# Down projection in seven block products: weight sums kept in eight tiles of their own, rings of six operand pairs

## The chip, the core and the metric

The kernel runs on one core of a Trainium2 chip. Its time is in device microseconds (us), the median over runs of the whole program; "profiled execution" means the one execution whose trace is quoted. The engines are PE (TensorE, matmul; PEld is its weight load), DVE (VectorE), ACT (ScalarE), POOL (GpSimd) and SP (SyncE, which here only issues DMAs). Each engine takes its instructions in the order in which they stand in its own queue.

## What is computed

One layer of a decoder for 2048 tokens of width 1024. Three mixers (dilated attention, a convolution module, a gated linear recurrence) share one input projection and one output projection, and a squared-ReLU MLP follows:

```python
mix = jnp.concatenate([y_attn, y_conv, y_lru], axis=-1)
x = x + jnp.einsum("bsc,cd->bsd", mix, w_out)
h2 = rmsnorm(x, norm2_g)
ff = jnp.square(jax.nn.relu(jnp.einsum("bsd,df->bsf", h2, w_up)))
return x + jnp.einsum("bsf,fd->bsd", ff, w_down)
```

A final RMSNorm ends it. All inputs are float32, and the change is in the last product, `ff @ w_down`, 4096 by 1024.

## The kernel before

**Precision.** Each float32 operand is split into a rounded high part and the remainder (`halves`: a cast on ACT, line 891, then a subtraction on DVE, line 892), and each product is made of three matmuls, high by high, high by low, low by high (lines 1427 to 1429 in the down stage).

**Halves of the tokens.** The tokens are worked in two halves `h` of 1024. Each half goes through the output projection (`outproj`), the up projection (`up`) and the down projection (`down`). The mixers of the second half run beside these stages of the first half: `tick` takes a piece of them after each batch of matmuls. In the profile the down stage of the first half lies at 964 to about 1300 us, that of the second half at 1718 to 2033 us.

**Seven products.** The down projection is cut into two-by-two blocks and done with seven block products instead of eight (`PRODUCTS`, in the order 1, 2, 7, 6, 4, 5, 3). The moving operand of a product is a sum of blocks of `ff`, which `up` has written to memory (`fscr`). The stationary operand is a block of `w_down` or a sum of blocks, which is made on DVE during the stage. Each product has eight steps, so the stage has 56 steps `g`; a step has 24 matmuls, on four PSUM banks.

**What a step needs.** For each step there is a pair S (high and low half of the moving operand, 128 by 1024 each) and a pair T (the same of the weights). They lie in 24 places `X(0)` to `X(23)`:

- S has a ring of three pairs (`S_AT`). `s_load(g + 2)` is issued in step g, so it waits until step g - 1 has freed the pair. `s_split(g + 1)` follows in the same step.
- T has a ring of nine pairs (`T_AT`). `ahead(g)` lets the splits run up to eight steps ahead of the matmuls, the sums one further and the loads three.
- Raw blocks of `w_down` come into a ring of seven tiles (`block0` to `block6`), taken in turn.
- `t_sum` makes the weights. Products 7 and 5 subtract one raw block from another (line 1292). Products 6 and 4 add or subtract the two rounded parts of the previous product's weights, two DVE operations each (line 1297).

```python
elif i in (6, 4):
    x = raws[t][0]
    op = nc.vector.tensor_add if i == 6 else nc.vector.tensor_sub
    for y in t_tiles(t - 8)[::-1]:
        op(x, x, f32(y))
```

**What sets the order.** The program text gives a first order and priorities; a scheduler then places each instruction in its engine's queue as early as its own reckoning allows. `with first()` gives the copies out of the PSUM banks (`evac`) priority. They stand at the end of each product: a bank has to be read before the next product writes it. Products 1 and 7 are copied by ACT (lines 1433, 1435), the others are added by DVE (lines 1437, 1440). A queue is not reordered at run time, so a copy waits for whatever stands ahead of it.

**The seam.** During the last product of the first half, `hooks` loads the mixers' results for the next output projection (`act_load`, into places 8 to 15) and splits them (`act_split`).

Of the kernel before, what the change touches and what calls it, by code (L numbers as in the profile page):

```python
# [38 lines left out]
T_AT = ((2, 3), (6, 7), (8, 9), (10, 11), (12, 13), (14, 15), (18, 19), (20, 21), (22, 23))  # L39
S_AT = ((0, 1), (4, 5), (16, 17))  # L40
# [37 lines left out]
def body(tc, xt, w_in, w_v, w_out, w_up, w_down, vecs, lru_wa, lru_wx, consts, out):  # L78
# [1173 lines left out]
    def down_steps(h):  # L1252
        raws, w = {}, {}

        def t_tiles(t):
            return [X(i) for i in T_AT[t % 9]]

        def s_tiles(g):
            return [X(i) for i in S_AT[g % 3]]

        def s_load(g):
            n, kp = divmod(g, 8)
            sh, sl = s_tiles(g)
            nc.sync.dma_start(f32(sl).rearrange("p (k n) -> p k n", k=2),
                              fscr[h, MOVING[PRODUCTS[n]], 2 * kp:2 * kp + 2].rearrange("k p n -> p k n"))
# [5 lines left out]
        def t_load(t, raw=None):  # L1271
# [3 lines left out]
            def block(a, b):  # L1275
                dst = raw()
                src = w_down[16 * a + 2 * kp:16 * a + 2 * kp + 2, :, b * NB:(b + 1) * NB]
                nc.sync.dma_start(dst.rearrange("p (k n) -> p k n", k=2), src.rearrange("k p n -> p k n"))
                return dst

            if i == 1:
                nc.sync.dma_start(f32(t_tiles(t)[1]).rearrange("p (k n) -> p k n", k=2),
                                  down_w[2 * kp:2 * kp + 2].rearrange("k p n -> p k n"))
            else:
                raws[t] = [block(*x) for x in {2: ((1, 0),), 7: ((1, 1), (0, 1)), 6: ((0, 0),), 4: ((1, 0),),
                                               5: ((0, 1), (0, 0)), 3: ((1, 1),)}[i]]

        def t_sum(t):
            i = PRODUCTS[t // 8]
            if i in (7, 5):  # L1290
                x, y = raws[t]
                nc.vector.tensor_sub(x, x, y)
            elif i in (6, 4):
                x = raws[t][0]
                op = nc.vector.tensor_add if i == 6 else nc.vector.tensor_sub
                for y in t_tiles(t - 8)[::-1]:
                    op(x, x, f32(y))

        def t_split(t):
            th, tl = t_tiles(t)  # L1300
            halves(raws.pop(t)[0] if t >= 8 else f32(tl), th, tl)

        return s_tiles, t_tiles, s_load, s_split, t_load, t_sum, t_split
# [335 lines left out]
```

## Time and profile before

| what | value |
|---|---|
| median of 3 runs | 2057.28 us (2055.09 to 2058.45) |
| the profiled execution, its own time | 2052.25 us |
| its span, first to last instruction | 2050.4 us |
| mean granted TensorE clock | 0.993 of full |
| DMA traffic | 416.32 MB, 203 GB/s mean |

The span is the time from the first instruction to the last; 1.85 us of the execution's own time lie around it. A row of a view gives an engine, the source line, the operation with its tiles (written before read), the count, and times. "Idle before" is the time in which the engine had nothing running, with what ended it. PE's matmuls overlap one another, so an idle time of PE is a little less than what was lost there.

### The profile page before, as it was taken

What the parts mean: (1) busy time and instruction counts of PE and PEld (TensorE: products, weight loads), DVE (VectorE), ACT (ScalarE), POOL (GpSimd) and SP (SyncE); (2) the same over time, 40 slices, a digit from 0 to 9 for tenths busy, and PEclk for the clock granted to TensorE, in tenths of its full rate; (3) what the DMA queues carried; (4) which work ended last, traced back from release to release, by engine and by line L of the source; (5) the groups of instructions that cost most, each with busy time, mean ns of one, the idle gap of its engine ahead of it and who ended that gap; (6) DMA issues with size and microseconds to landing.
All of it is one profiled execution on the core that took longest, in us unless ns stands there. A gap on an engine that the chain in (4) does not pass through costs nothing.

```text
span 2050.4 us, 25667 instructions
## 1 busy us (share of the span) xinstructions
PE 1974.6 (96%) x8876; PEld 1588.8 (77%) x8876; DVE 1501.0 (73%) x2009; ACT 1054.1 (51%) x1623; POOL 167.9 (8%) x296
## 2 busy tenths in 40 slices
PE   8999999999999999999998999989999999999997
PEld 6877777887777777887877778767888887887785
DVE  7899865577687667888898997677555555798755
ACT  6144875323667754566665554355545545444331
POOL 0113100000123322000000000100000000000000
PEclk9999999999999999999999999999999999999998
DMA  5555584833786547446995684785444448976734
GB/s 165 175 151 159 175 298 148 276 114 118 240 277 190 185 152 250 152 164 212 338 323 199 203 284 148 239 271 172 151 148 150 152 141 279 328 275 220 251 103 144
DMA packets 208750, 416.32 MB, mean 203 GB/s; under 512 B 26118, under 2 KB 34550, under 8 KB 208556
## 3 DMA queue, kind: packets, MB, share of 16 engines
q1 hardware_dynamic: 189204, 358.27, 52.2%
q0 software_dynamic: 16208, 45.91, 7.5%
q10 hardware_dynamic: 3208, 10.49, 1.5%
q8 instruction: 70, 1.15, 0.2%
q14 instruction: 60, 0.49, 0.1%
HBM read 299.79 MB, written 123.19 MB: 206 GB/s over the span
## 4 chain that ended last, share of the span: by engine, by line
PE 58%; issue 15%; DMA 13%; DVE 9%; ACT 4%; SPq 1%; POOL 1%; DVEq 0%; ACTq 0%; POOLq 0%
PE bank L1113 9%; PE bank L1114 9%; PE bank L1115 9%; PE bank L1428 4%; PE bank L1429 4%; PE bank L1427 4%; DMA rounded<-fscr 4%; PE mm L255 4%; PE mm L261 4%; PE mm L258 4%; DMA pair<-out_w 2%; DVE rounded L892 2%; DVE wide L462 1%; DMA m<-oscr 1%; DMA wraw<-in_w_up 1%
## 5 line engine op out<-in xcount | busy, mean ns | idle before, releaser
L1113 PE MATMUL bank<-rounded,pair 128*128 128x512 f32 x896 | 354.4, 396 | 1.8 <-ACT low L1193 1.7
L1114 PE MATMUL bank<-rounded,pair 128*128 128x512 f32 x896 | 352.9, 394 | 0.0
L1115 PE MATMUL bank<-rounded,pair 128*128 128x512 f32 x896 | 351.0, 392 | 0.0
L891 ACT CAST rounded<-rounded 128x1024 fp32r<-128x1024 f32 (+1 forms) x168 | 160.4, 967 | 316.9 <-DMA rounded<-fscr 256.3
L892 DVE TENSOR_TENSOR rounded<-rounded 128x1024 fp32r<-128x1024 f32 (+1 forms) x168 | 186.3, 1118 | 127.1 <-ACT rounded L891 126.7
L1427 PE MATMUL bank<-rounded,rounded 128*128 128x512 f32 x672 | 264.8, 395 | 10.7 <-ACT v L1435 5.5
L1428 PE MATMUL bank<-rounded,rounded 128*128 128x512 f32 x672 | 264.2, 393 | 5.3 <-DVE rounded L892 5.3
L1429 PE MATMUL bank<-rounded,rounded 128*128 128x512 f32 x672 | 263.3, 392 | 0.0
L1113 PEld LDWEIGHTS bank<-rounded,pair 128*128 128x128 f32 x896 | 168.2, 188 | 42.2 <-issue 2.6
L1115 PEld LDWEIGHTS bank<-rounded,pair 128*128 128x128 f32 x896 | 168.4, 188 | 37.4 <-issue 0.6
L1114 PEld LDWEIGHTS bank<-rounded,pair 128*128 128x128 f32 x896 | 168.4, 188 | 35.9 <-issue 0.7
L255 PE MATMUL mm<-rounded,rounded 128*128 128x512 f32 x496 | 160.8, 400 | 9.5 <-ACT rounded L235 7.5
L261 PE MATMUL mm<-rounded,rounded 128*128 128x512 f32 x496 | 159.7, 397 | 0.0
L1427 PEld LDWEIGHTS bank<-rounded,rounded 128*128 128x128 f32 x672 | 127.0, 189 | 41.3 <-ACT v L1435 6.9
L258 PE MATMUL mm<-rounded,rounded 128*128 128x512 f32 x496 | 158.6, 397 | 0.0
L1428 PEld LDWEIGHTS bank<-rounded,rounded 128*128 128x128 f32 x672 | 127.2, 189 | 34.6 <-DVE rounded L892 8.0
L1429 PEld LDWEIGHTS bank<-rounded,rounded 128*128 128x128 f32 x672 | 127.2, 189 | 26.6
L235 ACT CAST rounded<-raw 128x512 fp32r<-128x512 f32 (+1 forms) x96 | 55.9, 584 | 154.9 <-PE mm L258 110.8
L891 ACT CAST pair<-wraw 128x1024 fp32r<-128x1024 f32 x64 | 67.2, 1050 | 115.0 <-PE bank L1114 112.9
L892 DVE TENSOR_TENSOR rounded<-block,rounded 128x1024 fp32r<-128x1024 f32 x96 | 116.8, 1218 | 12.9 <-ACT rounded L891 12.0
L892 DVE TENSOR_TENSOR pair<-wraw,pair 128x1024 fp32r<-128x1024 f32 x64 | 78.2, 1222 | 62.9 <-ACT pair L891 61.7
L255 PEld LDWEIGHTS mm<-rounded,rounded 128*128 128x128 f32 x496 | 93.8, 190 | 32.0 <-ACT rounded L235 7.9
(320 smaller groups left out, 3773.0 us busy)
## 6 DMA issues: line engine op xcount, KB each, us to landing
block<-in_w_down SPq DMA_DIRECT2D x128, 512.0 KB, 5.7
fscr<-low SPq DMA_DIRECT2D x224, 256.0 KB, 2.2
rounded<-fscr SPq DMA_DIRECT2D x112, 512.0 KB, 4.9
raw<-in_w_in SPq DMA_DIRECT2D x64, 256.0 KB, 3.8
wraw<-in_w_up SPq DMA_DIRECT2D x64, 256.0 KB, 3.0
low<-in_w_up SPq DMA_DIRECT2D x64, 256.0 KB, 3.3
pair<-out_w SPq DMA_DIRECT2D x24, 512.0 KB, 5.9
raw<-in_xt SPq DMA_DIRECT2D x32, 256.0 KB, 3.6
```

The source lines that it names most:

```text
L235: nc.scalar.copy(h, raw)
L255: nc.tensor.matmul(bank, wh[:, sl], ah[:, cols], start=first_, stop=False)
L258: nc.tensor.matmul(bank, wh[:, sl], al[:, cols], start=False, stop=False)
L261: nc.tensor.matmul(bank, wl[:, sl], ah[:, cols], start=False, stop=last_)
L891: nc.scalar.copy(h, raw)
L892: nc.vector.tensor_sub(l, raw, f32(h))
L1113: nc.tensor.matmul(bank, wh[:, sl], hi(x), start=fresh and k == 0, stop=False, **kw)
L1114: nc.tensor.matmul(bank, wh[:, sl], lo(x), start=False, stop=False, **kw)
L1115: nc.tensor.matmul(bank, wl[:, sl], hi(x), start=False, stop=k == KH - 1, **kw)
L1427: nc.tensor.matmul(banks[j], th[:, c], sh[:, x], start=fresh and k0, stop=False, **kw)
L1428: nc.tensor.matmul(banks[j], th[:, c], sl[:, x], start=False, stop=False, **kw)
L1429: nc.tensor.matmul(banks[j], tl[:, c], sh[:, x], start=False, stop=k1, **kw)
```

## The change

S and T each get a ring of six pairs (`S_AT` with six entries, `T_AT` with six). The weight sums get eight tiles of their own, `kept0` to `kept7`, one for each step of a product, and each product's sum is made from the sum of the product before and one raw block: W7 = W(1,1) - W(0,1), W6 = W7 + W(0,0), W4 = W(1,0) - W6. Raw blocks that are only operands of a sum, or that are used as they are in product 3, come into three tiles `second0` to `second2`. In step g the program text asks for: S loads up to step g + 5, S splits up to g + 2, sums up to g + 3, T splits up to g + 2, block loads up to g + 5. The prologue in `up` loads a fourth S pair in place of a seventh T pair.

In the last product of the first half the loads of the mixers' results come later, since places 8 to 15 are now used until step 53, and their splits go in twos. The scratch space for software-made DMA descriptors goes from its default to 4096 bytes, which makes room for the additional tiles.

```diff
-T_AT = ((2, 3), (6, 7), (8, 9), (10, 11), (12, 13), (14, 15), (18, 19), (20, 21), (22, 23))
-S_AT = ((0, 1), (4, 5), (16, 17))
+T_AT = ((2, 3), (6, 7), (8, 9), (10, 11), (12, 13), (14, 15))
+S_AT = ((0, 1), (4, 5), (16, 17), (18, 19), (20, 21), (22, 23))
...
-                raws[t] = [block(*x) for x in {2: ((1, 0),), 7: ((1, 1), (0, 1)), 6: ((0, 0),), 4: ((1, 0),),
-                                               5: ((0, 1), (0, 0)), 3: ((1, 1),)}[i]]
+            if i in (2, 7, 5):
+                block(kept[kp], *{2: (1, 0), 7: (1, 1), 5: (0, 1)}[i])
+            if i in (7, 6, 4, 5, 3):
+                block(second[t % 3], *{7: (0, 1), 6: (0, 0), 4: (1, 0), 5: (0, 0), 3: (1, 1)}[i])
...
             if i in (7, 5):
-                x, y = raws[t]
-                nc.vector.tensor_sub(x, x, y)
-            elif i in (6, 4):
-                x = raws[t][0]
-                op = nc.vector.tensor_add if i == 6 else nc.vector.tensor_sub
-                for y in t_tiles(t - 8)[::-1]:
-                    op(x, x, f32(y))
+                nc.vector.tensor_sub(kept[kp], kept[kp], second[t % 3])
+            elif i == 6:
+                nc.vector.tensor_add(kept[kp], kept[kp], second[t % 3])
+            elif i == 4:
+                nc.vector.tensor_sub(kept[kp], second[t % 3], kept[kp])
...
         def ahead(g):
-            split = min(g + 8, 4 + 3 * (g + 1) // 2, 56)
...
+            for name, to, do in (("s load", 6, s_load), ("s split", 3, s_split), ("sum", 4, t_sum), ("split", 3, t_split), ("load", 6, t_load)):
+                while upto[name] < min(g + to, 56):
+                    do(upto[name])
+                    upto[name] += 1
...
-            if g + 2 < 56 and g:
-                s_load(g + 2)
-            if g + 1 < 56 and g:
-                s_split(g + 1)
             ahead(g)
...
-                act_load(1, 1, 0, 2)
             elif h == 0 and kp == 2:
-                act_load(1, 1, 2, 4)
-                act_load(1, 1, 4, 5)
                 out_load(0, state_["pairs"])
...
-    nc = bacc.Bacc("TRN2", target_bir_lowering=False, num_devices=1)
+    nc = bacc.Bacc("TRN2", target_bir_lowering=False, num_devices=1, dynamic_dma_scratch_size=4096)
```

**Where the queues change.** Three places, all in the first half. In the names, `rounded0`, `1`, `4` and `5` hold the S pairs that matter here, `rounded2` and `3` T pairs.

ACT, at the end of product 7 (step 23), where it copies the four banks into `v`. Before:

```order
L891 CAST rounded4_77<-rounded4_77 128x1024
L891 CAST rounded2_75<-block1_7673 128x1024
L891 CAST rounded2_75<-block2_7674 128x1024
L891 CAST rounded0_73<-rounded0_73 128x1024
L1435 COPY v_7690<-bank0_4017 128x512
L891 CAST rounded3_76<-block3_7675 128x1024
L1435 COPY v_7690<-bank1_4018 128x512
L891 CAST rounded1_74<-rounded1_74 128x1024
L1435 COPY v_7690<-bank2_4019 128x512
L1435 COPY v_7690<-bank3_4020 128x512
```

And with the change:

```order
L891 CAST rounded4_77<-rounded4_77 128x1024
L891 CAST rounded2_75<-kept3_7675 128x1024
L891 CAST rounded4_77<-rounded4_77 128x1024
L235 CAST mr_8634<-m_8560 128x512
L891 CAST rounded3_76<-kept4_7676 128x1024
L1431 COPY v_7691<-bank0_4017 128x512
L1431 COPY v_7691<-bank1_4018 128x512
L891 CAST rounded5_78<-rounded5_78 128x1024
L1431 COPY v_7691<-bank2_4019 128x512
L891 CAST rounded3_76<-kept5_7677 128x1024
L1431 COPY v_7691<-bank3_4020 128x512
```

Before, the S casts of steps 24 and 25 stand ahead of the first and the third copy. Now the S casts of steps 26 and 27 stand ahead of the first and that of step 28 ahead of the third: the casts have moved forward in the queue by as many steps as the ring grew.

SP, at the same place. The S loads in the first list are those of steps 23, 24 and 25 (`rounded4`, `rounded0`, `rounded1`); in the second list those of steps 25 (`rounded1`), 26 and 27 (`rounded4`) and 28 (`rounded5`). `block` and `second` are raw weights. Before:

```order
L1264 DMA rounded4_77<-fscr_117 128x2x512
L1278 DMA block0_7672<-in_w_down 128x2x512
L1264 DMA rounded0_73<-fscr_117 128x2x512
L1278 DMA block1_7673<-in_w_down 128x2x512
L1264 DMA rounded1_74<-fscr_117 128x2x512
```

And with the change:

```order
L1266 DMA rounded1_74<-fscr_117 128x2x512
L1279 DMA second1_7696<-in_w_down 128x2x512
L1279 DMA second2_7697<-in_w_down 128x2x512
L1279 DMA second0_7695<-in_w_down 128x2x512
L1279 DMA second1_7696<-in_w_down 128x2x512
L1266 DMA rounded4_77<-fscr_117 128x2x512 x2
L1266 DMA rounded5_78<-fscr_117 128x2x512
```

One block load stood ahead of each S load; now four, those of steps 28 to 31, stand ahead of three S loads in a row. The last of the three is the one whose cast stands between the copies.

DVE, at the end of product 2 (step 15), where it adds the banks into `z0`. Before:

```order
L1297 TENSOR_TENSOR block3_7675<-block3_7675,rounded5_78 128x1024
L1297 TENSOR_TENSOR block4_7676<-block4_7676,rounded5_78 128x1024
L1297 TENSOR_TENSOR block5_7677<-block5_7677,rounded0_73 128x1024
L557 TENSOR_TENSOR m_8135<-m_8135,m_8205 128x512
L1297 TENSOR_TENSOR block4_7676<-block4_7676,rounded5_78 128x1024
L1440 TENSOR_TENSOR z0_7683<-z0_7683,bank0_4017 128x512
```

And with the change:

```order
L892 TENSOR_TENSOR rounded1_74<-kept3_7675,rounded1_74 128x1024
L1294 TENSOR_TENSOR kept0_7672<-kept0_7672,second0_7695 128x1024
L1294 TENSOR_TENSOR kept1_7673<-kept1_7673,second1_7696 128x1024
L1294 TENSOR_TENSOR kept2_7674<-kept2_7674,second2_7697 128x1024
L557 TENSOR_TENSOR m_8123<-m_8123,m_8192 128x512
L1294 TENSOR_TENSOR kept3_7675<-kept3_7675,second0_7695 128x1024
L1436 TENSOR_TENSOR z0_7684<-z0_7684,bank0_4017 128x512
```

The sums for product 6, eight steps or more ahead of their use, still stand ahead of the first addition of `z0`. They are now one operation each, and each needs a raw block from the ring of three.

## Rows read from the trace of the kernel before

**Rows 1.** The page's busy times of the engines, of the whole span.

```profile
PE 1974.6 (96%) x8876; PEld 1588.8 (77%) x8876; DVE 1501.0 (73%) x2009; ACT 1054.1 (51%) x1623; POOL 167.9 (8%) x296
```

**Rows 2.** Stretches: busy time (instructions) by engine, granted clock, DMA share, GB/s.

```profile
core 0: us, PE busy (x) PEld busy (x) DVE busy (x) ACT busy (x) POOL busy (x), PEclk, DMA share, GB/s
1008.00:1052.00 44.00, 41.81 (x182) 33.73 (x181) 39.10 (x38) 27.07 (x32) 2.14 (x4) 1.00 0.98 348
1104.30:1114.20 9.90, 6.26 (x27) 4.62 (x25) 7.03 (x8) 1.73 (x4) 0.87 (x2) 0.98 0.93 304
1807.00:1851.00 44.00, 44.00 (x196) 36.28 (x195) 41.57 (x40) 18.00 (x21) 0.00 (x0) 1.00 0.70 246
```

**Rows 3.** PE's waits, whole span: for whom, us in total, times, longest.

```profile
PE bank L1428 <- DVE rounded L892: 7.5, 8, 1.4
...
PE bank L1427 <- ACT v L1435: 5.5, 2, 5.2
...
PE bank L1427 <- DVE z L1440: 2.4, 2, 1.9
PE bank L1427 <- DVE u L1437: 2.0, 2, 1.1
PE cb L552 <- ACT mr L235: 1.7, 2, 1.1
...
PE bank L1429 <- DVE rounded L892: 1.5, 2, 1.0
...
PE bank L1427 <- ACT rounded L891: 0.8, 1, 0.8
...
PE bank L1427 <- ACT u L1433: 0.8, 1, 0.8
```

**Rows 4.** Timeline of PE, the start of the second half's down stage.

```profile
1716.31 0.40 PE L1114 MATMUL bank<-rounded,pair 128*128 128x512 f32 x1
1716.54 0.40 PE L1115 MATMUL bank<-rounded,pair 128*128 128x512 f32 x1
1717.76 0.50 PE L1427 MATMUL bank<-rounded 128*128 128x512 f32 x1 [0.82 <-ACT rounded L891]
1718.10 0.40 PE L1428 MATMUL bank<-rounded 128*128 128x512 f32 x1
```

**Rows 5.** Two stretches of the down stages at the lower granted clock.

```profile
1113.89:1120.72 6.83, 4.95 (x12) 3.90 (x13) 5.46 (x6) 4.53 (x6) 0.00 (x0) 0.50 0.29 108
1943.33:1946.75 3.42, 3.42 (x9) 2.64 (x9) 2.70 (x4) 2.90 (x4) 0.00 (x0) 0.50 0.84 293
```

**Rows 6.** Timeline of ACT around the end of product 7, first half.

```profile
1108.28 0.57 ACT L1435 COPY v<-bank 128x512 f32<-128x512 f32 x1
1114.18 1.04 ACT L891 CAST rounded<-rounded 128x1024 fp32r<-128x1024 f32 x1 [5.33 <-DMA rounded<-fscr]
1115.13 1.06 ACT L1435 COPY v<-bank 128x512 f32<-128x512 f32 x2
```

**Rows 7.** Timelines of SP and of POOL just before.

```profile
1103.90 0.37 SPq L1278 DMA_DIRECT2D block<-in_w_down  x1
1104.36 0.46 SPq L1264 DMA_DIRECT2D rounded<-fscr  x1
...
1103.57 0.54 POOL L559 DMA_DIRECT2D m<-gscr  x1
1104.10 0.54 POOL L530 DMA_DIRECT2D m<-lscr  x1
1104.63 0.54 POOL L531 DMA_DIRECT2D mr<-gates_w  x1
```

**Rows 8.** DMA issues: count, KB each, median us to landing.

```profile
block<-in_w_down SPq DMA_DIRECT2D x128, 512.0 KB, 5.7
rounded<-fscr SPq DMA_DIRECT2D x112, 512.0 KB, 4.9
rounded<-mscr SPq DMA_DIRECT2D x8, 512.0 KB, 5.2
```

**Rows 9.** Groups of instructions, 1720 to 2050.4 us: busy, mean ns, idle before.

```profile
L1297 DVE TENSOR_TENSOR block<-block,rounded 128x1024 f32<-128x1024 f32 x32 | 38.1, 1215 | 1.2 <-DMA block<-in_w_down 1.1
```

**Rows 10.** POOL's largest group, whole span, and its DMA's time to landing.

```profile
L591 POOL DMA_DIRECT2D m<-zscr x48 | 28.9, 606 | 397.8 <-PE cb L709 195.9 <-DMA zscr<-z 79.4 <-PE mb L733 41.6
m<-zscr POOLq DMA_DIRECT2D x48, 128.0 KB, 4.0
```

More of the change, by code (lines that the diff above doesn't have):

```diff
@@ L1252, in down_steps, with two @@
     def down_steps(h):
-        raws, w = {}, {}
+        kept, second = [], []
         def t_tiles(t):
-            return [X(i) for i in T_AT[t % 9]]
+            return [X(i) for i in T_AT[t % 6]]
         def s_tiles(g):
-            return [X(i) for i in S_AT[g % 3]]
+            return [X(i) for i in S_AT[g % 6]]
+        def two(a):
+            return a.rearrange("p (k n) -> p k n", k=2)
         def s_load(g):
             n, kp = divmod(g, 8)
-            sh, sl = s_tiles(g)
-            nc.sync.dma_start(f32(sl).rearrange("p (k n) -> p k n", k=2),
+            nc.sync.dma_start(two(f32(s_tiles(g)[1])),
                               fscr[h, MOVING[PRODUCTS[n]], 2 * kp:2 * kp + 2].rearrange("k p n -> p k n"))
@@ L1299, in t_split @@
         def t_split(t):
+            n, kp = divmod(t, 8)
             th, tl = t_tiles(t)
-            halves(raws.pop(t)[0] if t >= 8 else f32(tl), th, tl)
-        return s_tiles, t_tiles, s_load, s_split, t_load, t_sum, t_split
+            halves(f32(tl) if n == 0 else second[t % 3] if PRODUCTS[n] == 3 else kept[kp], th, tl)
+        return s_load, s_split, s_tiles, t_load, t_sum, t_split, t_tiles, kept, second
     def down_prologue(steps):
-        s_tiles, t_tiles, s_load, s_split, t_load, t_sum, t_split = steps
+        s_load, s_split, s_tiles, t_load, t_sum, t_split = steps[:6]
@@ L1334, in down @@
     def down(h, steps, banks, hooks):
-        s_tiles, t_tiles, s_load, s_split, t_load, t_sum, t_split = steps
+        s_load, s_split, s_tiles, t_load, t_sum, t_split, t_tiles, kept, second = steps
         lp = pool(f"early{h}", 1, reuse_waits="tile")
-        raw = ring([lp.tile([P, HS], F32, name=f"block{i}") for i in range(7)])
+        kept.extend(lp.tile([P, HS], F32, name=f"kept{i}") for i in range(8))
         u = lp.tile([P, 4 * NB], F32, name="u")
@@ L1344, in down @@
         vv = rp.tile([P, 4 * NB], F32, name="v")
+        sp = pool(f"second{h}", 1, side="right", reuse_waits="tile")
+        second.extend(sp.tile([P, HS], F32, name=f"second{i}") for i in range(3))
         def part(t, j):
@@ L1562, in hooks @@
                 state_["pairs"] = left_pairs(1)
-                act_load(1, 1, 0, 2)
             elif h == 0 and kp == 2:
-                act_load(1, 1, 2, 4)
-                act_load(1, 1, 4, 5)
                 out_load(0, state_["pairs"])
-            elif h == 0 and kp == 3:
-                act_load(1, 1, 5, 8)
-                out_load(1, state_["pairs"])
-                act_split(1, 0)
             elif h == 0:
-                for n in range(2 * kp - 7, min(2 * kp - 5, 8)):
-                    act_split(1, n)
+                for n0, n1 in ((), ((0, 2),), ((2, 4),), ((4, 5), (5, 6)), ((6, 8),))[kp - 2] if kp < 7 else ():
+                    act_load(1, 1, n0, n1)
+                if kp == 3:
+                    out_load(1, state_["pairs"])
+                else:
+                    act_split(1, 2 * kp - 8)
+                    act_split(1, 2 * kp - 7)
                 if kp == 5:
@@ L1578, in body @@
         tail = down(h, steps, banks, hooks)
+        close(f"second{h}")
         if h:
```

30 lines of the change are left out of this document (9 added, 21 removed).

## The prediction

> **What bounds the kernel now.** I read the page's busy times first, then the busy times by stretch, then PE's waits, then the timelines at the longest wait. The kernel is bound by PE: it is busy 96% of the span [rows 1], and in an undisturbed stretch of the second half's down stage it is busy for all of 44.00 us [rows 2]. The change takes no matmul away. So it can only win back time in which PE stood still, and the question is how much of that belongs to the down stages.
>
> PE's waits of the down stages are those of lines 1427 to 1429 [rows 3]: 7.5 + 5.5 + 2.4 + 2.0 + 1.5 + 0.8 + 0.8 = 20.5 us in 18 waits. The waits of line 1429 (1.5 in two) and the one on an ACT cast (0.8) lie at the starts of the two stages, where the first operands come in; the change leaves these alone. That leaves 18.2 us in 15 waits, of two kinds:
> - **Split waits**, line 1428 on DVE's `rounded`: 7.5 us in 8. The low half of S comes too late for its step.
> - **Copy waits**, line 1427 on `v`, `z` and `u`: 5.5 + 2.4 + 2.0 + 0.8 = 10.7 us in 7. A bank of the finished product has not been read when the next product wants to write it.
>
> A wait costs more than its idle time, because matmuls overlap. Matmuls normally start 0.23 us apart [rows 4]. At a wait of 0.82 the starts are 1.22 apart, which is 0.99 lost, and the next interval is 0.34, another 0.11: 1.10 lost for 0.82, so 0.28 more per wait. And there are two stretches at the lower clock level of 1.2 GHz (granted 0.50) [rows 5]. The first begins inside the longest copy wait, so PE had stood still before it; in it matmuls run for 4.95 us, of which half, 2.5, is lost. The second loses half of 3.42, 1.7. I put both, 4.2, to the copy waits; only the first is shown to belong there.
>
> Split waits: 7.5 + 8 x 0.28 = **9.7**. Copy waits: 10.7 + 7 x 0.28 + 4.2 = **16.9**. Together 26.6 us, 1.3% of the span, can be won.
>
> **How the longest wait comes about.** At the end of product 7, ACT has copied the second bank at 1108.28, then stands 5.33 us for a DMA, casts that S tile at 1114.18 and copies the last two banks at 1115.13, while PE waits 5.2 us for them [rows 3, 6]. The cast is that of step 25, and stands ahead of the copies in ACT's queue, as the order shows. Its load was issued at 1104.36, behind a block load at 1103.90, so it took 9.8 us to land, against a median of 4.9 [rows 7, 8]. Just then POOL issued three loads for the mixers [rows 7], and the DMA engines were busy for 0.93 of 1104.30 to 1114.20 [rows 2]. So this wait is a late landing of an S load, handed on by the order of ACT's queue.
>
> **The change, part by part.**
>
> *S ring of six, splits two steps ahead.* An S load is issued when the matmuls of six steps before are done, instead of three. A step is 24 x 0.23 = 5.5 us, so each operand has 16.5 us more. Even the longest landing, 9.8, is inside that. The split waits go: **-9.7**. Bounds: nothing, if the casts now wait elsewhere for just as long; 9.7. I take all of it, since 16.5 is far over the longest row.
>
> *Copies.* Here the ring does less than it seems. The order shows that the casts moved forward in ACT's queue by the same three steps: ahead of the third copy of product 7 there stood the cast of step 25, whose pair step 22 frees, and now there stands that of step 28, whose pair step 22 frees too. So the S load that the copy waits for starts no earlier than before. What is there for it: from the end of step 22, one step (5.5) and two banks of the next one (12 x 0.23 = 2.8) pass before PE wants the third bank; a cast of 1.04 and a copy of 0.57 [rows 6] come off, which leaves 6.6 us for the landing. The median lands in 4.9 [rows 8], and 9.8 does not fit. Before, one block load stood ahead of each S load on SP, and at the costly place one was issued 0.46 us ahead of it [rows 7], itself waiting for a raw tile. Now the four ahead of it need sums that DVE's queue has some ten steps earlier, so they should be gone when the pair comes free. DVE also has 16 fewer sums in each half, 16 x 1.215 = 19.4 us [rows 9]; they lie beside PE's work and count for nothing themselves, but the copies by DVE (4.4 us of the waits) stand behind less. Bounds: nothing goes (the gate is the same), or all 16.9 goes. I take two thirds, **-11.3**, because the slack is nearer to the common landing than to the rare one.
>
> *Loads.* As many blocks and S tiles as before. In 1008 to 1052 the DMA share was 0.98 [rows 2]; the old text asked there for one and a half T pairs a step, the new one asks for one. I cost this at nothing.
>
> *Raw blocks in three tiles.* A block load now waits for the sum of three steps before. At the end of product 2 four sums for product 6 stand in DVE's queue ahead of the first addition into `z0`, and each needs its raw block. If the last one comes late, PE waits there. The nearest rows are the waits for `z` and `u`, up to 1.9 and 1.1 [rows 3]; before, the same sums took two operations each, so part of the wait is old. I take **+0.9**, bounds 0 and 3 (one raw landing of 5.7 [rows 8] less half a step).
>
> *The seam.* The mixers' loads of the next output projection now wait for steps 50 to 53. They land in 5.2 [rows 8], the splits follow before step 55 ends (two steps, 11 us, less 5.2, a cast of 1.04 [rows 6] and a subtraction, which I take as long as a sum of the same shape, 1.215 [rows 9]): 3.5 us to spare. Cost 0; the bound is one whole landing with both, 7.5.
>
> *PE's queue and POOL's queue* keep their order. The mixers' waits (1.7 in two [rows 3], 2.3 with the extra) may go or stay: 0.
>
> **Sum:** -9.7 - 11.3 + 0.9 = -20.1. The profiled execution took 2052.25 of its own time, with a span of 2050.4, and would take 2032.2. It lies 5.0 under the median of the runs; against the median I forecast 2057.3 - 20.1 = **2037** us.
>
> **Rivals.**
> - *The copies stay as they are.* The gate is the same and the casts stand ahead of the copies, so the copy waits keep their place and price; only the split waits go. 2057.3 - 9.7 = 2047.6. For it: the order. Against it: the slack of 6.6 over the median landing.
> - *Slower: S loads held on SP.* Four block loads stand ahead of three S loads. If the third raw tile comes free late (DVE is busy 39.10 of 44 us in the first half [rows 2]), SP stands, the S loads behind it start late, and bank copies stall at the price of the longest wait, 5.2 + 0.28 + 2.5 = 8.0 each. The old copy waits would stay too. There are 12 product ends with a successor; the point from which it is slower is 9.7 / 8.0, so two of them: -9.7 + 16.0 = +6.3, 2063.6. Against it: at every place that I followed in the order, the sum that frees the tile stands well ahead.
> - *The copies stay and the seam is late.* With the 7.5 at the seam in full: 2047.6 + 7.5 = 2055.1, no change. For it: the first half ends with DVE and ACT on the last operands. Against it: the 3.5 us to spare.
> - *The smaller descriptor ring holds POOL.* POOL issues a DMA in 0.606 us and it lands 4.0 later [rows 10], so some seven are under way at a time. If the ring were too small for that and each had to land first, each would cost 3.4 more; 296 instructions of POOL [rows 1] make 1006 us, and if a tenth of it reaches PE, +100, 2157. The share is a guess; POOL is idle 92% of the time [rows 1]. The Trainium skill, "DMA: Bandwidth & Descriptors", section "SWDGE vs HWDGE vs iDMA", says that the descriptors of DMAs issued from GpSimd are written by software into rings kept in reserved SBUF, and "SBUF — State Buffer", section "SBUF size: 192, 224, or 256?", gives that reserve as 16 KiB per partition; the change leaves 4096 bytes. Neither says what happens when it fills, and no run so far shows a smaller one.
>
> **Numbers.** My forecast 0.58; copies stay 0.22; S loads held 0.09; no change by the seam 0.08; descriptor ring 0.03. The first two are faster: 0.80. No change, within 0.2% or 4.1 us, which is about what a measurement of this kernel can tell: 0.08. Slower: 0.12. The range: its low end is all 26.6 and the mixers' 2.3 gone, 2028; its high end is the split waits alone less the 3 of a late raw block, 2057.3 - 6.7 = 2050. That leaves out the last three cases, 0.20. My own case alone gives 2028 to 2044 (a third of the copy waits gone and 0.9 lost: 9.7 + 5.6 - 0.9 = 14.4, so 2043).
>
> **What would show it.** Right: no waits of line 1428 on DVE inside the stages; copy waits of 6 us or less with their surplus, in fewer than seven; no half-clock stretch at the end of product 7; at most one new wait for `z` at the end of product 2. The same copy waits with the S cast ahead of them mean the first rival. SP's block loads late, with S loads issued right behind them, mean the second. A wait on `rounded` at the second half's `outproj` means the seam. POOL's DMAs 4 us apart mean the ring. I am wrong altogether if the gain comes from other stages, or if the time moves by over 4 us with PE's waits of lines 1427 to 1429 unchanged.

## The result and the profile after

| | kernel before | the change |
|---|---|---|
| median, five runs each on one chip | 2055.09 us (2054.51 to 2058.45) | 2044.68 us (2037.72 to 2047.68) |
| ratio of the times | | 0.9938, 95% interval 0.9914 to 0.9961 |
| once more, 16 and 7 runs | 2052.68 us | 2039.52 us, ratio 0.9935 (0.991 to 0.996) |
| the profiled execution, its own time | 2052.25 us | 2037.72 us (second profile 2039.24) |
| first half's down stage, first to last matmul start | 339.34 us | 330.48 (332.01) |
| second half's down stage | 315.13 us | 306.20 (306.20) |

The ratio makes 0.0062 x 2055.09 = 12.7 us, with 8.0 and 17.7 at the ends of its interval. The two down stages together are 17.8 us shorter in the profile (654.47 to 636.68). The profiled execution, the fastest of the five, is 14.5 shorter than that of the kernel before. Most of the difference between 17.8 and 14.5 lies ahead of the first half's down stage, which begins 3.1 us later (967.80 instead of 964.67); there the program text differs only in the prologue in `up`. In the 14 profiles of this study that start lies anywhere from 963.0 to 972.1, so whole runs vary by several us before the down stages begin. The stage lengths are the finer measure, and they are used below beside the medians.

The page's busy times answer to [rows 1]:

```profile
PE 1966.7 (97%) x8876; PEld 1587.4 (78%) x8876; DVE 1466.1 (72%) x1977; ACT 1053.8 (52%) x1623; POOL 168.4 (8%) x296
```

The same number of matmuls. DVE has 32 instructions less and 34.9 us less, 1.1 us each. The busy times by stretch, where the first and third stretch answer to [rows 2], the second is the place of the longest wait now, and the last is the half-clock stretch behind it, as in [rows 5]:

```profile
core 0: us, PE busy (x) PEld busy (x) DVE busy (x) ACT busy (x) POOL busy (x), PEclk, DMA share, GB/s
1008.00:1052.00 44.00, 42.74 (x189) 34.98 (x188) 33.30 (x34) 24.58 (x29) 2.14 (x4) 1.00 0.99 355
1140.00:1162.00 22.00, 16.54 (x72) 13.33 (x71) 16.33 (x16) 7.99 (x10) 1.62 (x4) 0.98 0.89 293
1807.00:1851.00 44.00, 44.00 (x195) 36.41 (x194) 36.20 (x30) 19.12 (x21) 0.00 (x0) 1.00 0.80 283
1161.14:1164.56 3.42, 3.24 (x8) 2.57 (x9) 1.92 (x4) 3.16 (x5) 0.00 (x0) 0.50 0.85 305
```

The DMA engines are as full in 1008 to 1052 as before (0.99, before 0.98), and DVE has 33.30 instead of 39.10 there. PE's waits in the down stages answer to [rows 3]; lines 1427 to 1429 are now 1423 to 1425:

```profile
PE bank L1423 <- DVE u L1433: 5.5, 1, 5.5
...
PE bank L1423 <- DVE z L1436: 1.6, 2, 1.3
...
PE bank L1423 <- ACT u L1429: 1.3, 1, 1.3
PE bank L1425 <- DVE rounded L892: 1.1, 1, 1.1
...
PE bank L1423 <- ACT v L1431: 0.7, 1, 0.7
```

The split waits (8 of line 1428, 7.5 us) have no row any more; the one on `rounded` is at a stage's start. The copy waits are still there: 5.5 + 1.6 + 1.3 + 0.7 = 9.1 us in five, all in the first half. Before they were 10.7 in seven, 7.5 of it in the first half. So the second half's stage has lost every wait and the first half's copy waits are longer than they were. The longest has moved from the end of product 7 to the end of product 6.

What SP waited for in 1120 to 1165, and three timelines of SP, ACT and DVE ahead of that wait of PE, show it (`kept` and `second` are raw weights or their sums).

```profile
SPq L1279 <- DVE rounded L892: 21.2, 5, 8.1
```

```profile
1132.46 0.36 SPq L1266 DMA_DIRECT2D rounded<-fscr  x1
1140.99 1.46 SPq L1279 DMA_DIRECT2D kept<-in_w_down  x2
1142.55 0.63 SPq L1266 DMA_DIRECT2D rounded<-fscr  x1
1143.27 0.77 SPq L1279 DMA_DIRECT2D second<-in_w_down  x1
1149.20 0.37 SPq L1279 DMA_DIRECT2D kept<-in_w_down  x1
1149.66 0.42 SPq L1266 DMA_DIRECT2D rounded<-fscr  x1
```

```profile
1151.27 1.05 ACT L891 CAST rounded<-rounded 128x1024 fp32r<-128x1024 f32 x1 [11.12 <-DMA rounded<-fscr]
...
1156.09 1.04 ACT L891 CAST rounded<-rounded 128x1024 fp32r<-128x1024 f32 x1 [2.83 <-DMA rounded<-fscr]
```

```profile
1146.81 1.22 DVE L1292 TENSOR_TENSOR kept<-kept,second 128x1024 f32<-128x1024 f32 x1 [2.48 <-DMA kept<-in_w_down]
...
1149.97 1.23 DVE L1292 TENSOR_TENSOR kept<-kept,second 128x1024 f32<-128x1024 f32 x1 [0.80 <-DMA kept<-in_w_down]
1152.35 1.23 DVE L892 TENSOR_TENSOR rounded<-rounded 128x1024 fp32r<-128x1024 f32 x1 [1.16 <-ACT rounded L891]
...
1157.17 1.23 DVE L892 TENSOR_TENSOR rounded<-rounded 128x1024 fp32r<-128x1024 f32 x1 [1.13 <-ACT rounded L891]
...
1159.45 1.22 DVE L1292 TENSOR_TENSOR kept<-kept,second 128x1024 f32<-128x1024 f32 x1
1160.58 1.28 DVE L1433 TENSOR_TENSOR u<-u,bank 128x512 f32<-128x512 f32 x2
```

SP issues nothing for 8 us and then three block loads and the S load of step 34 within 3.1 us. The two `kept` loads in front are blocks of steps 40 and 41, and stand directly ahead of that S load in SP's queue. They wait for DVE: a `kept` tile comes free when the weights in it have been split. The S pair of step 34 had been free since step 28 ended at 1138.09, 4.45 us before its load went out. POOL issues the three mixers' loads at 1140.56 to 1141.62, at the same moment. ACT casts the S tile of step 34 only 8.7 us after the issue of its load, and has waited 11.12 for it. The S load of step 35 goes out at 1149.66, 6.13 us after its pair came free and again directly behind a `kept` load.

DVE has weight sums and splits in its queue ahead of the addition of the finished banks into `u`. From 1144 on it stands still four times: 2.48 and 0.80 us for the `kept` blocks of steps 40 and 41, 1.16 and 1.13 us for the casts of steps 34 and 35. That is 5.57 us in sum, and the addition comes only at 1160.58. PE stands still for 5.46 us, though step 34 itself begins only at 1173.91. So it is the chain of [rows 6, 7], with SP's order added, and in this profile late block loads have a larger part in it than late S loads.

### The profile page after: what moved, and what is told of

Same layout as the page of the kernel before. It is cut to its first block, busy times and chain, and to the rows that moved or that the text cites. A ratio compares the mean times of both kernels' runs of the same rounds, so it can differ in the third digit from the quotient of the medians.

```text
span 2035.9 us, 25608 instructions
## 1 busy us (share of the span) xinstructions
PE 1966.7 (97%) x8876; PEld 1587.4 (78%) x8876; DVE 1466.1 (72%) x1977; ACT 1053.8 (52%) x1623; POOL 168.4 (8%) x296
## 4 chain that ended last, share of the span: by engine, by line
PE 73%; DMA 11%; DVE 9%; ACT 4%; issue 3%; SPq 1%; DVEq 0%; POOL 0%; ACTq 0%
PE bank L1113 9%; PE bank L1114 9%; PE bank L1115 9%; PE bank L1423 8%; PE bank L1424 8%; PE bank L1425 8%; PE mm L255 4%; PE mm L258 4%; PE mm L261 3%; DMA rounded<-fscr 2%; DMA pair<-out_w 2%; DMA raw<-in_xt 2%; DVE wide L462 1%; DVE rounded L892 1%; PE bank L929 1%
## 5 line engine op out<-in xcount | busy, mean ns | idle before, releaser
L1423 PE MATMUL bank<-rounded,rounded 128*128 128x512 f32 x576 | 225.4, 391 | 8.4 <-DVE u L1433 5.5
L1425 PE MATMUL bank<-rounded,rounded 128*128 128x512 f32 x576 | 224.7, 390 | 0.0
L1424 PE MATMUL bank<-rounded,rounded 128*128 128x512 f32 x576 | 224.7, 390 | 0.0
L1423 PEld LDWEIGHTS bank<-rounded,rounded 128*128 128x128 f32 x576 | 108.5, 188 | 32.9 <-DVE u L1433 6.1
L1423 PE MATMUL bank<-rounded 128*128 128x512 f32 x320 | 125.5, 392 | 0.7 <-ACT v L1431 0.7
L1424 PEld LDWEIGHTS bank<-rounded,rounded 128*128 128x128 f32 x576 | 108.6, 188 | 22.6
L1425 PEld LDWEIGHTS bank<-rounded,rounded 128*128 128x128 f32 x576 | 108.4, 188 | 22.7
L1425 PE MATMUL bank<-rounded 128*128 128x512 f32 x320 | 124.7, 390 | 1.1 <-DVE rounded L892 1.1
L1424 PE MATMUL bank<-rounded 128*128 128x512 f32 x320 | 124.6, 389 | 0.0
```

The costliest lines, as they stand in the source:

```text
L1423: nc.tensor.matmul(banks[j], th[:, c], sh[:, x], start=fresh and k0, stop=False, **kw)
L1424: nc.tensor.matmul(banks[j], th[:, c], sl[:, x], start=False, stop=False, **kw)
L1425: nc.tensor.matmul(banks[j], tl[:, c], sh[:, x], start=False, stop=k1, **kw)
```

## Experiments

The table gives for each the median, its ratio to the kernel before on the same chip, and the two down stages of one profile. The kernel before had a median of 2052.68 us beside runs 1 to 4, 2056.27 beside runs 5 to 8 and 2054.89 beside runs 9 to 12. Without the time that PE lost in them (each interval of over 0.24 us between two matmul starts, less the normal 0.227), the stages are 314.7 to 315.2 and 305.2 to 305.5 us long in all 14 profiles. So every difference between stages below is time in which PE stood still or ran at the lower clock.

| run | median us | ratio (95%) | first half | second half |
|---|---|---|---|---|
| the change again | 2039.52 | 0.9935 (0.991 to 0.996) | 332.01 | 306.20 |
| sums only | 2042.83 | 0.9951 (0.9933 to 0.9969) | 337.54 | 308.99 |
| S splits behind copies | 2038.99 | 0.9933 (0.9909 to 0.9956) | 330.10 | 307.31 |
| all splits and sums behind copies | 2034.17 | 0.9919 (0.9894 to 0.9945) | 329.69 | 307.00 |
| block loads behind S loads | 2030.45 | 0.9879 (0.9859 to 0.9899) | 321.91 | 306.64 |
| POOL's three loads cut | 2024.31 | 0.9846 (0.9824 to 0.9868) | 321.00 | 307.13 |
| change with three S pairs | 2045.21 | 0.9946 (0.9931 to 0.9961) | 332.02 | 310.97 |
| before, small scratch space | 2055.00 | 1.0 (0.9986 to 1.0013) | 341.15 | 315.26 |
| sums only, made twice | 2041.31 | 0.9938 (0.9916 to 0.996) | 329.55 | 312.95 |
| before, POOL's three loads cut | 2044.35 | 0.9953 (0.9932 to 0.9974) | 329.45 | 314.18 |
| four S pairs, block loads behind S loads | 2025.37 | 0.9863 (0.9839 to 0.9886) | 321.06 | 306.20 |
| both rules of order | 2024.92 | 0.9864 (0.984 to 0.9889) | 319.80 | 306.20 |

**1. The change again.** No edit.

> The changed kernel once more, unaltered, to see which part of its time varies. Its five times spread over 10 us (2037.72 to 2047.68), before's over 4. Theory (the copies behind a late S load are a matter of timing): the second half's down stage takes 306 us again within 1, and the spread is in the first half, where the copy wait at the end of product 6 (5.5 us in the first profile) or another of the first half's product ends comes in another size, 0 to 12 us. Rival (the spread comes from elsewhere, from the stages before 960 us): the first half's down stage takes 330 to 331 again, and the stretch before it, 967.8 in the first profile, differs by several us. Median 2038 to 2048 in both.

The second half is the same to 0.01 us; the first half's wait at the end of product 6 comes again, 7.9 us this time, after the same pattern on SP. It is no accident of one execution. The start of the stage differs by 2 us between the two profiles and the first half's stage by 1.5, so both add to the spread of the runs; how much each does, two profiles cannot tell.

**2. Sums only.** The kept tiles and the three raw tiles of the change, with before's rings.

```diff
+T_AT = ((2, 3), (6, 7), (8, 9), (10, 11), (12, 13), (14, 15), (18, 19), (20, 21), (22, 23))
+S_AT = ((0, 1), (4, 5), (16, 17))
...
-            for name, to, do in (("s load", 6, s_load), ("s split", 3, s_split), ...
+            for name, to, do in (("s load", 3, s_load), ("s split", 2, s_split), ...
```

> S in a ring of three pairs, loaded and split as before, T in nine pairs; only the weight sums are those of the change (eight kept tiles, three raw ones, one operation). Theory (the longer S ring takes the split waits away): the split waits are all back, about 7 to 10 us in 8 or so, second half included; the time is within 4 us of the kernel before, 2051 to 2058. Rival (16 fewer sums in each half relieve DVE, and that is the gain): the split waits go here too, and the time is that of the change, 2040 to 2046.

Both expectations were half wrong. PE's waits of this run:

```profile
PE bank L1423 <- DVE rounded L892: 10.7, 7, 5.4
```

The split waits are there with three S pairs, as the theory has it, but nearly all of them (six of seven) in the first half. In the second half the sums alone take 6.1 of the 8.9 us. The time is 10.0 under before's (0.0049 x 2052.68), most of what the change brings.

**3. S splits behind the copies.** A rule of order, no wait: an S cast or subtraction may not pass a bank copy of its own engine that stands earlier in the program.

```diff
+                    if name == "s split":
+                        held(lambda: do(upto[name]), (mybir.EngineType.DVE, mybir.EngineType.Activation))
+                    else:
+                        do(upto[name])
```

> The change, with one rule for the order: the cast and the subtraction of an S pair may not stand ahead of a bank copy that comes before them in the program text. Theory (S casts and subtractions ahead of the copies hand a late S load on to PE): the copy waits of the first half, 9.1 us in five in the first profile of the change, fall to 2 or less, no half-clock stretch follows a product's end, and the profile is 8 to 12 us shorter than that of the change with like stages before, the median 2030 to 2038. Rival (the copies wait for block loads: DVE's sums ahead of them need kept tiles that land late): the wait at the end of product 6 stays above 4 us, the median within 4 us of the change.

My theory fell, and what the rival forecast came: the wait at the end of product 6 is 8.0 us here. The rival's reason is a part of it. DVE's sums for product 5 still stand ahead of the additions into `u`, and one of them stands 2.99 us for its kept tile. Splits of weights stand there too, and one waits 3.46 us for its cast, which ACT makes only after the cast of a late S tile. ACT copies no bank of product 6, so the rule holds back no S cast there:

```profile
1152.56 1.05 ACT L891 CAST rounded<-rounded 128x1024 fp32r<-128x1024 f32 x1 [7.08 <-DMA rounded<-fscr]
```

```profile
1149.90 1.23 DVE L1292 TENSOR_TENSOR kept<-kept,second 128x1024 f32<-128x1024 f32 x1 [2.99 <-DMA kept<-in_w_down]
1154.59 1.22 DVE L892 TENSOR_TENSOR rounded<-kept,rounded 128x1024 fp32r<-128x1024 f32 x1 [3.46 <-ACT rounded L891]
...
1160.89 1.28 DVE L1451 TENSOR_TENSOR u<-u,bank 128x512 f32<-128x512 f32 x2
```

**4. All splits and sums behind the copies.** The same rule for everything that `ahead` gives to ACT and DVE (`if True` in place of `if name == "s split"`).

> As the run before it, with sums and T splits held behind the copies too. Theory: nothing more to win, the same median within 3 us (2030 to 2038); if the sums held there were part of the wait, 1 to 4 us better. Rival (work that is held back comes too late for its own step): new waits of lines 1423 to 1425's matmuls on DVE's splits behind each product's end, 1 to 3 us each at some of 12 ends, 5 to 20 us slower than with the S splits held alone.

The copy waits are gone, and the stage is as long as before. PE now waits for the mixers, in another line:

```profile
PE cb L552 <- ACT mr L235: 5.4, 2, 3.7
PE cb L553 <- DVE mr L236: 2.4, 1, 2.4
```

These are 7.8 us, at 1084, 1120 and 1186. In each case the mixers' operation stands behind one that waits for a load: behind S casts of ACT that wait 3.71 and 5.49 us, and behind a sum of DVE that waits 3.79. Whatever is put first, something stands still, which pointed to a cause ahead of ACT and DVE, in the loads. The rival's waits were expected on the splits and came in another row; slower, as it had forecast, the run is not (329.69 us against 330.10).

**5. Block loads behind S loads.** The rule on SP's queue: a block load may not pass an S load that stands earlier in the program.

```diff
+        def load_held(t):
+            start = len(nc.cur_bb.bb.instructions)
+            t_load(t)
+            for i in nc.cur_bb.bb.instructions[start:]:
+                if s_last:
+                    tc.add_manual_dep(i, s_last[0].name, mybir.DependencyInfo(
+                        mybir.DependencyClass.NoSync, mybir.DependencyReason.DATA), reason="step")
+
+        def s_load_kept(g):
+            s_load(g)
+            s_last[:] = [nc.cur_bb.bb.instructions[-1]]
```

**6. POOL's three loads cut.** The change with its own order, and less data at the moment of the collision.

```diff
-                loads(h).dma_start(x[:, :n + 3], lscr[t][:, t0 + 29:t0 + n + 32])
-                loads(h).dma_start(gw.bitcast(F32), gates_w[t])
+                few = 16 if h else P
+                if h:
+                    nc.gpsimd.memset(x, 0.0)
+                    nc.gpsimd.memset(gw.bitcast(F32), 0.0)
+                loads(h).dma_start(x[:few, :n + 3], lscr[t][:few, t0 + 29:t0 + n + 32])
+                loads(h).dma_start(gw.bitcast(F32)[:few], gates_w[t][:few])
...
-                loads(h).dma_start(gg, gscr[t][:, t0:t0 + n])
+                if h:
+                    nc.gpsimd.memset(gg, 0.0)
+                loads(h).dma_start(gg[:few], gscr[t][:few, t0:t0 + n])
```

> The change, with one rule for SP's order: a block load may not stand ahead of an S load that comes before it in the program text. In the changed kernel S of step 34 was issued 4.45 us after its pair was free, behind two loads into kept tiles and with a third and a fourth load in the same 2 us, and the copies at the end of product 6 cost 5.5 and 7.9 us in two profiles. Theory A (block loads hold SP, then go out in a bunch): S loads go out within 0.5 us of their pair's end, the wait at the end of product 6 falls below 2 us, the first half's down stage takes 321 to 326 us instead of 330.5 and 332.0, and the median is 2029 to 2035. Theory B (three loads that POOL issues for the mixers at the same moment fill the DMA engines, so S lands late whenever it goes out): the wait stays above 4 us, the stage at 328 to 333, the median at 2036 to 2043.

> The change, but POOL's three loads of a recurrence step of the second half's mixers bring 16 of 128 partitions (the rest of these tiles is set to zero), so that they put an eighth of the bytes on the DMA engines; the recurrence of the second half computes with zeros there. Theory A (SP held): no difference to speak of, wait at the end of product 6 above 4 us, first half's down stage 328 to 333 us, median 2036 to 2043. Theory B (POOL's three loads): the wait falls below 2 us, the stage to 321 to 326, the median to 2029 to 2035.

For the stage each theory's own run gave what it had forecast, and what each forecast for the other's run was wrong. With the rule, SP's timeline at the same place is even, one S load a step (of 5.44 us; the one between these two is left out):

```profile
1131.51 0.37 SPq L1266 DMA_DIRECT2D rounded<-fscr  x1
...
1142.39 0.37 SPq L1266 DMA_DIRECT2D rounded<-fscr  x1
```

POOL's three loads come as ever, at 1140.80 to 1141.86, and the stretches at that place show PE busy without a break:

```profile
1136.00:1146.00 10.00, 10.00 (x46) 8.29 (x45) 10.00 (x12) 4.27 (x5) 2.14 (x4) 1.00 0.74 218
1146.00:1162.00 16.00, 16.00 (x72) 13.15 (x72) 11.32 (x12) 8.60 (x10) 0.00 (x0) 1.00 0.59 197
```

The DMA share is 0.74 and 0.59; over 1140 to 1162 it is 0.68, against 0.89 in the change. S loads go out more than 0.6 us late in 2 of 50 steps of the first half (6.6 us in sum), against 14 (58.7) in the change and 9 of 53 (17.1) in the kernel before. Without POOL's bytes, in run 6, S loads still go out up to 2.3 us late (4.4 at step 6, as in the change), so a part of the lateness comes from the collision itself; no wait is longer than 1.8. So with six S pairs it takes both to make the long wait: block loads held up on SP that then go out in a bunch, and POOL's loads at that moment. Taking away either takes 8.6 to 11.0 us off the first half's stage (330.48 and 332.01 to 321.91 or 321.00). Run 6 is shorter elsewhere too, since these loads come in other stages as well; only its stage is compared. POOL also fills the three tiles with zeros there, so that its loads follow 0.3 to 1.3 us later than in the change behind the store ahead of them; that their bytes and not this shift are what counts is likely, and not shown.

A long wait can come without POOL's loads all the same. In run 2, with three S pairs, PE's longest wait is 5.36 us and ends at 1133.02, in step 27. The S tile of this step was cast in time, but its subtraction stands in DVE's queue behind a weight sum:

```profile
1130.15 1.22 DVE L1292 TENSOR_TENSOR kept<-kept,second 128x1024 f32<-128x1024 f32 x1 [5.07 <-DMA second<-in_w_down]
1131.29 0.54 DVE L536 TENSOR_SCALAR m<-m,vec 128x512 f32<-128x512 f32 x1
1131.75 1.22 DVE L892 TENSOR_TENSOR rounded<-rounded 128x1024 fp32r<-128x1024 f32 x1
```

Three block loads and an S load had gone out together there, at 1123.37 to 1125.09. POOL's loads had gone out at 1105.61 to 1106.67, and the next came at 1142.71.

**7. The change with three S pairs.** As run 2, but T in six pairs.

```diff
+S_AT = ((0, 1), (4, 5), (16, 17))
```

> The change with the S ring cut back to three pairs, loaded two steps ahead and split one ahead; T in six pairs as in the change. It differs from the run with only the sums changed in T's ring alone (six instead of nine pairs). Theory (the S ring brings the half of the gain that the sums do not): split waits of 6 us or more come back, both down stages together 643 to 649 us as with the sums alone (646.5; the change 636.7 and 638.2), median 2042 to 2049. Rival (it is the shorter T ring that spreads the loads): 634 to 640 us, median 2036 to 2042.

Together 643.0 us, the theory's lower edge: split waits are back (9.3 us in 8), in both halves. Against run 2, which differs in T's ring alone, the first half is 5.5 us shorter, without the split wait of 5.4, and the second 2.0 us longer. So T's ring of six may help in the first half and cost a little in the second; single profiles can't settle it.

**8. Before, with the small scratch space.**

```diff
+    nc = bacc.Bacc("TRN2", target_bir_lowering=False, num_devices=1, dynamic_dma_scratch_size=4096)
```

> The kernel before, with only the scratch space for software-made descriptors cut to 4096 bytes. Theory (seven DMAs under way fit): down stages 654 us together within 3, POOL's bunched DMAs 0.53 to 0.61 us apart, median 2049 to 2057. Rival (the ring fills): POOL's DMAs some 4 us apart, 2100 or more.

No difference, and POOL's group and its landings read as in [rows 10]:

```profile
L591 POOL DMA_DIRECT2D m<-zscr x48 | 28.9, 606 | 398.9 <-PE cb L709 196.1 <-DMA zscr<-z 78.5 <-PE mb L733 41.9
m<-zscr POOLq DMA_DIRECT2D x48, 128.0 KB, 3.9
```

**9. Sums only, made twice.** Run 2 with each sum of products 6 and 4 done twice.

```diff
                 nc.vector.tensor_add(kept[kp], kept[kp], second[t % 3])
+                nc.vector.tensor_add(kept[kp], kept[kp], second[t % 3])
```

> The run with only the sums changed (down stages 337.5 and 309.0 us, together 646.5; the kernel before 339.3 and 315.1), and each sum of products 6 and 4 made twice, so that DVE does as many operations as before; the weights of these products come out as other sums. It tells what of the sums' gain is DVE's time and what the order or the buffers. Theory (the gain of the sums is DVE's 19.4 us in each half): the second half's down stage is back at 313 to 316 us, the two together at 651 to 657, median 2048 to 2056. Rival (sums from a kept tile no longer wait for the parts of the T pair of eight steps before, and the loads go out in another order): 307 to 311 in the second half, together 644 to 649, median 2039 to 2047.

Inconclusive as to the whole. The second half goes from 309.0 to 312.95, two thirds of the way back to 315.1, with split waits again; so there about two thirds of what the sums had won are DVE's time. The first half is 8.0 us shorter than in run 2, mainly because this execution has no wait like that of 5.36 us in step 27, and the ratios are the same within their intervals. The change of the sums' order and buffers is not excluded as a part of the gain.

**10. Before, with POOL's three loads cut.** The edit of run 6.

> The kernel before, with POOL's three loads of a recurrence step of the second half's mixers cut to 16 of 128 partitions, as in the run with the change; the recurrence of the second half computes with zeros there. Theory (the 9.8 us landing at the end of product 7 came from these loads): the copy wait of 5.2 us there falls below 1.5 us and the half-clock stretch behind it goes, the split waits stay at 5 us or more; the first half's down stage 339.3 to 328 to 333 us, the second half's 315 within 1.5. Rival (S with three pairs is late by itself): the wait stays above 3 us, the stage at 335 to 341.

The wait on `v`, 5.2 us before, is 0.8, no half-clock stretch follows, and the stage is 9.9 us shorter, as expected; split waits of 3.4 us in four are left in it, fewer than the 5 expected. So in the kernel before too these 10 us need POOL's loads. Its S load at that place was issued 2.4 us after its pair was free, behind one block load [rows 7]; no run takes that away from the kernel before, so SP's part is not shown there.

**11. Four S pairs,** with the rule of run 5.

```diff
+S_AT = ((0, 1), (4, 5), (16, 17), (18, 19))
```

> The change with the rule for SP's order (no block load ahead of an earlier S load) and an S ring of four pairs instead of six. With n pairs a load has n - 1 steps from its gate to its use: 10.9 us with three, 16.3 with four, 27.2 with six. Theory (only the longest landing, 9.8 us, and a cast and a subtraction, 12.1 us together, must fit): no split waits, both down stages together 626 to 632 us as with six pairs (628.6), median 2028 to 2035. Rival (queue order eats the margin too): split waits of 2 to 6 us in the first half, together 632 to 638, median 2034 to 2041.

No split wait, 627.3 us together: once the loads go out in time, four pairs do what six do, and two pairs of places, four tiles, stay free in the stage.

**12. Both rules of order.**

> The change with both rules: no block load ahead of an earlier S load on SP, no S cast or subtraction ahead of an earlier bank copy. With the first rule alone one copy wait of 2.8 us and its half-clock stretch were left in the first half (stage 321.9, of it 7.0 lost), at the end of product 7, behind an S cast. Theory (that cast is the cause): this wait goes, the first half's stage 316 to 320, median 2024 to 2030. Rival (what is held behind the copies comes back as a wait elsewhere, as with all splits held): 320 to 325, median within 3 us of 2030.5.

The fastest by the stages, 626.0 us together. The first half's stage is in the theory's range, but its reason does not hold. The wait on `v` is still there, 1.2 instead of 2.8, and in the timeline of ACT in run 5 what stands ahead of the copies is the cast of a weight tile, which waits for DVE's sum. That cast waits 4.36 us in run 11 too and 4.30 here; no run changes the order of DVE ahead of that sum.

```profile
PE bank L1440 <- ACT v L1463: 1.2, 1, 1.2
```

```profile
1110.62 1.04 ACT L891 CAST rounded<-kept 128x1024 fp32r<-128x1024 f32 x1 [4.36 <-DVE kept L1294]
1111.58 1.07 ACT L1445 COPY v<-bank 128x512 f32<-128x512 f32 x2
```

Against the kernel before it wins 1.36%, where the change wins 0.62 to 0.65%. The intervals of runs 5, 11 and 12 overlap, so the medians do not tell what the second rule or the shorter ring is worth. Four pairs with both rules was not tried.

## Why the prediction was right, and where not

The forecast was faster, 2037 us in 2028 to 2050; the median is 2044.68, and the second set gives 2039.52. The direction and the bound (PE, with its waits in the down stages alone) were right. The gain was 17.8 us in the down stages and 10 to 13 in the medians, against 20.1 forecast. The range also covers a rival; the prediction's own case, 2028 to 2043 by its sum, holds the second median and not the first, though the kernel before came out at 2055.09 and not at the 2057.3 from which it counted. That 17.8 lies so near to 20.1 is in part luck: the copies won 6.5 us less than forecast, and 3.3 us came from elsewhere, mostly from places that the prediction had put at nothing. By the steps:

- *Split waits, -9.7.* Right in size: none is left in either profile of the change. The reason was half of it. Runs 2 and 7 show that the longer S ring is needed for the first half; in the second half most of the gain came with the sums.
- *DVE's 19.4 us "count for nothing themselves".* Wrong. The sums alone bring 7.9 us in the down stages and 10.0 in the medians. Run 9 puts 4 us of the second half to DVE's time. A split made late by DVE's queue is a wait of PE, as the longest one of run 2 shows, and I had counted only the copies as standing behind it.
- *Copies, -11.3.* This is the step that failed. In the second half the three waits went. In the first they are 9.1 us in five instead of 7.5 in four. By the prediction's own price 9.1 + 5 x 0.28 + half of the 3.24 us that matmuls ran at the lower clock = 12.1 is left of 16.9, a gain of 4.8. In the second profile of the change it is 14.3 (10.5 in three waits, and half of 5.99 us at the lower clock), a gain of 2.6. What was wrong in it was the sentence that the block loads ahead of an S load "should be gone when the pair comes free". I had followed the loads into the three raw tiles, whose sums are early, and not those into the kept tiles, which wait for the split of the step eight before. They are the two loads at 1140.99.
- *S loads held on SP,* with 0.09, was the rival whose mechanism came: S loads up to 6.7 us late, and one product end at 5.5 + 0.28 + 1.6 = 7.4 us, close to its price of 8.0 (11.2 in the second profile). It came once in each profile, and its point of decision was two; once was not enough to be slower, since the split waits had gone. What it had not seen is that the late block loads themselves stop DVE, for 3.28 of the 5.57 us above.
- *POOL's three loads.* The prediction read them rightly as the cause of the 9.8 us landing [rows 7], which run 10 confirms, and then took it as a rare landing. They come again and again in the first half (in the second profile of the change at 1104.81 and at 1139.00), and with six pairs it is their meeting a bunch on SP that makes the long wait.
- *The casts ahead of the copies* looked like the cause, and are one way in which it reaches PE: runs 3 and 4 change the order of ACT and DVE, and the loss only moves.
- *The new stall at the end of product 2, +0.9,* is 0.3 (the shorter of the two waits on `z`). *The seam, 0:* from the last matmul of the one down stage to the first of the other it is 413.75 us before and 413.98 after, 415.92 in the second profile; in all 14 it is 410.5 to 415.9, so a cost of a few us there would not show. *The mixers' waits of 1.7* went, and one of 0.7 on line 276 came. *The descriptor ring:* run 8 shows no cost.
- The terms with what was measured, -9.7 - 4.8 - 1.3 (the mixers' 1.7 + 2 x 0.28, less 0.7 + 0.28), make 15.8 of the 17.8. Another 0.8 is a wait at the start of the second half's stage, 0.53 with its surplus, which the prediction had expected to stay and the change does not have. The rest is in intervals that are a little longer than normal and that the views list under no wait.

## What to carry to other kernels

A deeper ring for one operand moves its loads, casts and splits forward together, so what stands behind them in the in-order queues stays where it was: ask of each queue what is ahead of the thing that the bound engine waits for, the queue that issues the DMAs first. When a loss comes back in another line after each reordering, as in runs 1, 3 and 4, look for a common cause further upstream. And compare the stage's own length, here good to 1 us where no long wait falls, when whole runs vary by several.

## What the runs showed that was not expected

That, with six S pairs, the collision needs both partners: the held loads or POOL's loads taken away, each alone, gave back 8.6 to 11.0 us of the stage.

The lower clock level also follows short stops. The timeline of PE in run 5, behind the wait on `v`, shows matmuls 0.43 us apart instead of 0.23 until 1115.35; the granted clock of that stretch is 0.50:

```profile
1112.21 0.80 PE L1437 MATMUL bank<-rounded 128*128 128x512 f32 x1 [2.75 <-ACT v L1445]
1112.80 0.63 PE L1438 MATMUL bank<-rounded 128*128 128x512 f32 x1
1113.23 0.63 PE L1439 MATMUL bank<-rounded 128*128 128x512 f32 x1
...
1115.35 0.39 PE L1438 MATMUL bank<-rounded 128*128 128x512 f32 x1
```

```profile
1111.90:1115.31 3.41, 3.10 (x7) 2.48 (x8) 3.41 (x5) 3.18 (x6) 0.00 (x0) 0.50 0.95 345
```

The 14 profiles have eleven waits of 1.84 to 2.75 us in a down stage. Eight of them, in six profiles, were followed by such a stretch, at a cost of about 1.6 us each; behind three, of 2.05 us in run 7, 2.39 in run 4 and 2.23 in run 8, there was none. The second stretch of [rows 5], which stood behind a copy wait of 1.9 us, is gone with that wait.
